# Layer A of a hybrid encoder: small products in groups, query norms from transposes, 128-row meta products, decays as rows from DRAM

## The chip, the core and the metric

The kernel runs on one core of a Trainium2 chip. The metric is the device time of one execution, in microseconds (us). The engines are PE (matmul) with its weight loads PEld, DVE (vector), ACT (scalar functions), POOL, and SP, which issues the DMAs. DRAM is the chip's large memory; SBUF and PSUM are the memories at the engines, PSUM the one that PE writes.

## The reference

The model is a trunk of two layers over 1024 tokens of width 1024 (plus 16 learned meta tokens ahead of them). Layer A is a gated delta rule with 8 heads of width 128; a shared latent key/value set is built from its output; layer B is latent attention. The change is in layer A alone:

```python
z = h @ w_in                                  # h: rms-normed input
qkv = silu(causal_dwconv(z[..., :3*1024], conv_w))
q = l2_norm(q) * 128 ** -0.5;  k = l2_norm(k)
beta = sigmoid(b_raw)
g = -exp(a_log) * softplus(a_raw + dt_bias)   # log decay per token and head
# gated_delta_rule, by chunks of tokens:
gc = cumsum(g)
decay = exp(where(tril, gc[:, None] - gc[None, :], -inf))
kb = k * beta
lower = where(tril_strict, (kb @ k.T) * decay, 0)
sol = triangular_solve(lower + eye, [v * beta, kb * exp(gc)])
attn = where(tril, (q @ k.T) * decay, 0)
# scan over chunks with the state S:
u = u_base - w_dec @ S
o = (q * exp(gc)) @ S + attn @ u
S = S * exp(gc_last) + (k * exp(gc_last - gc)).T @ u
```

Afterwards `o` is normed per head, multiplied with a gate, projected and added to the input.

## The kernel before

Tokens lie in tiles of 128, with the 16 meta tokens as a short tile ahead (tile -1, its values in column NT = 8 of the per-token tables). All float32 matmuls on weights are done as three products of split halves (`mm3`, L91 to L93, names `whi`, `wlo`, `hT_hi`, `hT_lo`). Other float32 products on 128 columns appear in the trace as two records each, transposes as one.

Layer A begins with the norm and transposition of the input (L250 to L259), the small projection for beta and decay (L264 to L287, on 32 columns of PE), and the per-token tables `beta`, `g`, `egc`, `ekd`, `egl` (L295 to L333). After that the work goes by pairs of heads. For every head, `conv_acts` makes keys, values and queries: 72 big matmuls in three chunks of tokens, and the convolution on POOL (L372) and DVE (L375). `key_prep` (L383) transposes the keys (L397), takes their squared sums on ACT, builds the decay matrix `att`, multiplies it with keys times keys (L440) into `U`, and sends `U` and the scaled betas through DRAM (`blk_in`, `beta_scr`). `invert_blocks` loads them as 66 blocks of 32x32 (`M`) and inverts them with 62 operations on DVE (L524, L527); `finish_inverses` assembles 128-row inverses with small products (names `fin`). `query_prep` takes the query norms and multiplies keys with queries. `scan_meta` and `scan_tile` run the recurrence: five products a tile and head (L611, L615, L616, L621, L625), with four results that DVE makes between them.

The decay matrix before is made by PE: for each pair of tiles POOL masks the split decay rows `ghi` and `glo` with a select (L429), PE sums them with the triangular matrix `after_r` (L431), ACT takes the exponential, and POOL selects the triangle again (L435). The query norms are sums over partitions: ACT squares the transposed queries, and PE multiplies each tile with a column of ones (L475).

The program order gives priorities, and a scheduler that works with modelled durations makes each engine's instruction list from them, so the lists interleave the pairs: the scan of one pair, the key preparation of the next and the conv matmuls of the one after share PE. Each list is executed in order. `att` has six buffers (two a head), `o`, the scan's result, three. All DMAs of layer A are issued by SP, in one queue; a DMA that waits holds up those behind it.

## Time and profile before

| | |
|---|---|
| Time, median of 3 runs | 1352.13 us (1349.76 to 1353.17) |
| Profiled execution, its own time | 1351.8 us |
| Its span | 1350.1 us |
| Mean granted TensorE clock | 0.989 |
| PE, DVE, ACT, POOL busy | 97%, 67%, 40%, 31% |

The span is the time that the profile covers; the execution's own time is 1.7 us longer. A row of a group gives the line, the engine, the operation, the output and input names, shapes and count, then busy time and the mean of one in ns, then the idle time before it and what ended it. A matmul's duration overlaps with its neighbours', so what one costs in the stream is read from the distance of starts, or from the busy time, in which overlaps are shared out.

### The profile page before, as it was taken

To read this page: it belongs to the slowest core of one execution; us is meant where nothing else is said; L and a number is where in the kernel's file an instruction comes from. 1 tells how busy PE (TensorE), PEld (TensorE's weight loads), DVE (VectorE), ACT (ScalarE), POOL (GpSimd) and SP (SyncE) were. 2 spreads that over 40 slices of the span, in tenths; PEclk is the share of its full clock that TensorE was granted. 3 is DMA by queue.
4 is the path that set the end of the run, shared out by engine and by line. 5 is a ranking of instruction groups with operands and counts; after the bars stand their busy time and mean duration, and the time that the engine had idled before them with its cause. 6 is when DMAs were issued, how large, how long until landed. Compare 5 with 4: busy or idle time off the path is not lost.

```text
span 1350.1 us, 24895 instructions
## 1 busy us (share of the span) xinstructions
PE 1306.3 (97%) x9064; PEld 1181.7 (88%) x9064; DVE 900.1 (67%) x2601; ACT 534.8 (40%) x1694; POOL 412.8 (31%) x680
## 2 busy tenths in 40 slices
PE   6999999999999999999999999998999999998998
PEld 4879989989998999997888798887999999998876
DVE  6669879968978884633553765224888878788221
ACT  6442343244325322211222243116777677776100
POOL 3344224323421320060101402212535435347000
PEclk9999999999999999999999999999999999999999
DMA  6111202111211113255441302311111101014443
GB/s 185 41 25 48 56 20 62 40 42 37 59 49 32 50 32 96 72 159 178 145 147 68 95 1 84 121 47 57 44 38 35 56 21 36 21 36 149 133 124 125
DMA packets 116924, 96.81 MB, mean 72 GB/s; under 512 B 28462, under 2 KB 106094, under 8 KB 116802
## 3 DMA queue, kind: packets, MB, share of 16 engines
q1 hardware_dynamic: 116802, 95.23, 23.7%
q8 instruction: 71, 1.16, 0.4%
q14 instruction: 51, 0.42, 0.1%
HBM read 68.19 MB, written 27.01 MB: 71 GB/s over the span
## 4 chain that ended last, share of the span: by engine, by line
PE 75%; DVE 8%; DMA 5%; POOL 5%; ACT 4%; issue 3%; SPq 0%; DVEq 0%; ACTq 0%; POOLq 0%
PE mm L91 7%; PE mm L93 7%; PE mm L92 7%; PE sc L93 6%; PE sc L92 6%; PE sc L91 6%; PE bd L91 3%; PE bd L93 3%; PE bd L92 3%; PE pt L1312 2%; PE tr L483 1%; DMA raw<-in_a_w_out 1%; ACT junk L82 1%; DMA out<-raw 1%; PE ch L625 1%
## 5 line engine op out<-in xcount | busy, mean ns | idle before, releaser
L91 PE MATMUL mm<-hT_hi,whi 128*128 128x384 f32 (+1 forms) x768 | 256.8, 334 | 3.5 <-DVE whi L98 3.5
L93 PE MATMUL mm<-hT_hi,wlo 128*128 128x384 f32 (+1 forms) x768 | 255.3, 332 | 0.7 <-DVE wlo L99 0.7
L92 PE MATMUL mm<-hT_lo,whi 128*128 128x384 f32 (+1 forms) x768 | 255.7, 333 | 0.0
L91 PEld LDWEIGHTS mm<-hT_hi,whi 128*128 128x128 f32 x768 | 147.4, 192 | 5.5 <-issue 4.7
L93 PEld LDWEIGHTS mm<-hT_hi,wlo 128*128 128x128 f32 x768 | 147.5, 192 | 2.5 <-DVE wlo L99 1.3
L92 PEld LDWEIGHTS mm<-hT_lo,whi 128*128 128x128 f32 x768 | 147.2, 192 | 1.4 <-issue 0.4
L108 DVE TENSOR_TENSOR pTl<-pt,pTh 128x256 fp32r<-128x256 f32 (+2 forms) x112 | 55.0, 494 | 11.0 <-ACT pTh L107 9.5
L98 POOL TENSOR_SCALAR whi<-raw 128x512 fp32r<-128x512 f32 x48 | 37.7, 799 | 70.4 <-PE mm L92 63.8
L82 ACT ACTIVATE P<-P,mx 128x144 f32<-128x144 f32 (+3 forms) x64 | 50.6, 791 | 21.8 <-DVE mx L1270 19.0
L91 PE MATMUL sc<-wo_hi,oTh 128*128 128x512 f32 (+1 forms) x144 | 57.5, 400 | 0.6 <-issue 0.6
L93 PE MATMUL sc<-wo_hi,oTl 128*128 128x512 f32 (+1 forms) x144 | 57.2, 397 | 0.0
L92 PE MATMUL sc<-wo_lo,oTh 128*128 128x512 f32 (+1 forms) x144 | 56.9, 395 | 0.0
L375 DVE SCALAR_TENSOR_TENSOR kn<-z,pcol,kn 128x384 f32<-128x384 f32 (+1 forms) x72 | 41.4, 576 | 19.4 <-POOL kn L372 18.8
L1283 POOL TENSOR_SCALAR P<-P,sl 128x144 f32<-128x144 f32 (+3 forms) x64 | 53.0, 829 | 3.7
L370 ACT COPY z<-mm 128x384 f32<-128x384 f32 (+1 forms) x72 | 31.8, 442 | 54.4 <-PE mm L93 54.3
L107 ACT CAST pTh<-pt 128x256 fp32r<-128x256 f32 (+2 forms) x112 | 47.3, 427 | 14.1 <-PE pt L1312 8.0
L99 DVE TENSOR_TENSOR wlo<-raw,whi 128x512 fp32r<-128x512 f32 x64 | 47.1, 746 | 8.5 <-POOL whi L98 8.4
L93 PE MATMUL sc<-h_hi,wlo 128*128 128x512 f32 x128 | 50.8, 397 | 0.0
L92 PE MATMUL sc<-h_lo,whi 128*128 128x512 f32 x128 | 50.6, 396 | 0.0
L91 PE MATMUL sc<-h_hi,whi 128*128 128x512 f32 x128 | 50.5, 395 | 0.0
L91 PE MATMUL bd<-wf_hi,oTh 128*128 128x512 f32 x128 | 50.2, 392 | 0.3 <-ACT oTh L1422 0.2
L102 DVE SCALAR_TENSOR_TENSOR wlo<-raw,pcol,whi 128x128 fp32r<-128x128 f32 x64 | 23.4, 429 | 40.0 <-POOL whi L101 40.0
(380 smaller groups left out, 3951.1 us busy)
## 6 DMA issues: line engine op xcount, KB each, us to landing
raw<-in_a_w_in SPq DMA_DIRECT2D x64, 256.0 KB
xt<-in_x SPq DMA_DIRECT2D x16, 512.0 KB
o_scr<-o SPq DMA_DIRECT2D x64, 64.0 KB
raw<-in_a_w_out SPq DMA_DIRECT2D x8, 512.0 KB
on<-o_scr SPq DMA_DIRECT2D x8, 512.0 KB
x_scr<-xt SPq DMA_DIRECT2D x8, 512.0 KB
raw<-in_b_w_in SPq DMA_DIRECT2D x8, 512.0 KB
gb_scr<-z SPq DMA_DIRECT2D x8, 512.0 KB
```

Source lines behind the costliest of these rows:

```text
L82: i = A.activation(out_ap, in_ap, func, **kw)
L91: TE.matmul(ps, ahi, bhi, start=first, stop=False)
L92: TE.matmul(ps, ahi, blo, start=False, stop=False)
L93: TE.matmul(ps, alo, bhi, start=False, stop=last)
L98: eng.tensor_scalar(out=hi, in0=raw, scalar1=1.0, scalar2=1.0, op0=ALU.mult, op1=ALU.mult)
L99: V.tensor_tensor(out=lo, in0=raw, in1=hi, op=ALU.subtract)
L107: A.copy(hi, ps)
L108: V.tensor_tensor(out=lo, in0=ps, in1=hi, op=ALU.subtract)
L370: A.copy(z[:, 3 + a:3 + b], gemm_T(hi, lo, c))
L375: V.scalar_tensor_tensor(out=yc, in0=z[:, a + j:b + j], scalar=col("cw", 24 * j + m), in1=yc, op0=ALU.mult, op1=ALU.add)
L1283: G.tensor_scalar(out=Pm[:, 0:n], in0=Pm[:, 0:n], scalar1=s, scalar2=1.0, op0=ALU.mult, op1=ALU.mult)
L1312: TE.transpose(pt[:, kb, x * P:(x + 1) * P], Ps[x][0][:, y0 + kb * P:y0 + (kb + 1) * P], ident)
```

## The change

The change touches layer A only; the part behind it has the same instructions. It does this:

- **Decays.** Instead of masked sums on PE, the sums of log decays per token are made once for all heads and tiles (`around` products), transposed, and written to DRAM (`r_scr`). Each head reads its rows back, broadcast to all partitions, into `att` (two DMAs of 256 KB a head). POOL masks it, adds the column sums `nb`, and ACT takes the exponential. The meta decays come from `rmb` and `nrm` in the same manner.
- **Query norms.** PE transposes the queries (9 products a head), and ACT squares and sums them from PSUM, as for the keys.
- **Scaled betas.** They are stored to `beta_scr` straight from their columns, 1024 pieces of four bytes a head, without transposes and copies.
- **Meta products** work on 128 rows with zeros in the rows that are not used; the small projection's weights are widened to 128 columns.
- **Order.** In `key_prep` the four transposes of a bank stand ahead of their four squares; in `scan_tile` the product with the queries stands right behind the one with the keys, and the one with `att` right behind the one with `kd`.

```diff
             sc = sp.tile([P, NT + 1], F32, tag="ksc", name=nm("ksc"))
             for half, s4 in halves() + [(2, slice(NT, NT + 1))]:
...
-                for j, t in enumerate(tiles):
-                    a, b = tok(t)
-                    TE.transpose(ps[0:k, j, :], kn[:, a:b], ident)
-                    act(junk[0:k], ps[0:k, j, :], AF.Square, accum_out=sk[0:k, s4.start + j, hc])
...
+                for j in range(n):
+                    a = tok(s4.start + j)[0] if half < 2 else 0
+                    TE.transpose(ps[:, j, :], kn[:, a:a + P], ident)
+                for j in range(n):
+                    act(junk, ps[:, j, :], AF.Square, accum_out=sk[:, s4.start + j, hc])
...
-            TE.transpose(ps[0:NT, 0:P], flat(br[:, 0:NT, hc]), ident)
-            TE.transpose(ps[0:1, P:P + NM], br[:NM, NT, hc], ident[:NM, :NM])
-            V.tensor_copy(brow, ps[0:NT, 0:P])
-            V.tensor_copy(browm, ps[0:1, P:P + NM])
-            SY.dma_start(beta_scr[h, NM:].rearrange("(t p) -> t p", p=P), brow)
-            SY.dma_start(beta_scr[hc, 0:NM], browm)
+            SY.dma_start(beta_scr[h, NM:].rearrange("(t p) -> p t", p=P), flat(br[:, 0:NT, hc]))
+            SY.dma_start(beta_scr[h, 0:NM], br[:NM, NT, hc])
...
+            for half in range(2):
+                SY.dma_start(flat(att[half]), r_scr[hc, 512 * half:512 * half + 512].broadcast_to([P, 512]))
...
             for half, s4 in halves():
-                ps = bank("tr", [P, 512])
-                for i in range(2):
-                    s2 = slice(s4.start + 2 * i, s4.start + 2 * i + 2)
-                    gs = [bp.tile([P, 2, P], F32R, tag=f"g{y}", name=nm("gm")) for y in range(2)]
-                    for y, gy in enumerate((ghi, glo)):
-                        G.affine_select(out=gs[y], in_=gy[:, s2, hc].broadcast_to([P, 2, P]), compare_op=ALU.is_ge,
-                                        fill=0.0, base=0, pattern=[[0, 2], [1, P]], channel_multiplier=-1)
-                        TE.matmul(ps[:, 256 * i:256 * i + 256], after_r, flat(gs[y]), start=y == 0, stop=y == 1)
-                act(flat(att[half]), ps, AF.Exp)
+                G.affine_select(out=att[half], in_=att[half], compare_op=ALU.is_ge, fill=MASKED, base=0,
+                                pattern=[[0, 4], [1, P]], channel_multiplier=-1)
+                a4 = att[half].rearrange("p t (c i) -> p (t c) i", c=2)
+                n4 = nb[:, h, s4].rearrange("p t c -> p (t c)")
+                G.tensor_tensor(out=a4, in0=a4, in1=n4[:, :, None].broadcast_to([P, 8, P // 2]), op=ALU.add)
+                act(flat(att[half]), flat(att[half]), AF.Exp)
...
-            for a, b in TOKC:
-                act(sq[:, a:b], qT[:, a:b], AF.Square)
-            for t in range(-1, NT):
-                a, b = tok(t)
-                s = t if t >= 0 else NT
-                TE.matmul(ps[0:b - a, s:s + 1], sq[:, a:b], one, start=True, stop=True)
+            for s4 in (slice(0, 4), slice(4, 8), slice(NT, NT + 1)):
+                ps = bank("tr", [P, 4, P])
+                junk = sp.tile([P, P], BF16, tag="jk", name=nm("junk"), bufs=1)
+                for j in range(s4.stop - s4.start):
+                    a = tok(s4.start + j)[0] if s4.start < NT else 0
+                    TE.transpose(ps[:, j, :], qT[:, a:a + P], ident)
+                for j in range(s4.stop - s4.start):
+                    act(junk, ps[:, j, :], AF.Square, accum_out=qss[:, s4.start + j:s4.start + j + 1])
...
             TE.matmul(ps[:, 0:P], c["kn"][:, a:b], S, start=True, stop=True)
+            TE.matmul(ps[:, 2 * P:3 * P], c["qT"][:, a:b], S, start=True, stop=True)
...
-            TE.matmul(ps[:, 2 * P:3 * P], c["qT"][:, a:b], S, start=True, stop=True)
...
                 TE.matmul(ps[:, 0:P], c["kd"][t // 4][:, t % 4, :], u, start=True, stop=True)
+            TE.matmul(ps[:, 3 * P:4 * P], c["att"][t // 4][:, t % 4, :], u, start=True, stop=True)
...
-            TE.matmul(ps[:, 3 * P:4 * P], c["att"][t // 4][:, t % 4, :], u, start=True, stop=True)
```

The scheduler's lists change all through layer A. PE first, in the scan of the first pair, where the keys of head 3 are transposed. In the names, `ch` are the scan's products, `mm` the conv matmuls, `tr` the others. Before:

```order
L91 MATMUL mm_473_2685<-hT_hi,whi_267_1876 128x384
L621 MATMUL ch_292_2026<-u_294_2032,kd_151_893 128x128
L397 MATMUL tr_428_2435<-ident,kn_272_1887 128x128
L92 MATMUL mm_473_2685<-hT_lo,whi_267_1876 128x384
L625 MATMUL ch_286_2008<-u_288_2014,att_108_753 128x128
L93 MATMUL mm_473_2685<-hT_hi,wlo_268_1877 128x384
L397 MATMUL tr_428_2435<-ident,kn_272_1887 128x128
L91 MATMUL mm_474_2716<-hT_hi,whi_267_1876 128x384
L397 MATMUL tr_433_2456<-ident,kn_272_1887 128x128
L92 MATMUL mm_474_2716<-hT_lo,whi_267_1876 128x384
```

And now:

```order
L92 MATMUL mm_425_2626<-hT_lo,whi_249_1879 128x384
L93 MATMUL mm_425_2626<-hT_hi,wlo_250_1880 128x384
L91 MATMUL mm_425_2626<-hT_hi,whi_249_1879 128x384
L92 MATMUL mm_425_2626<-hT_lo,whi_249_1879 128x384
L644 MATMUL ch_304_2119<-u_306_2125,kd_114_802 128x128
L645 MATMUL ch_304_2119<-u_306_2125,att_112_800 128x128
L634 MATMUL ch_310_2137<-S_301_2111,kn_107_704 128x128
L635 MATMUL ch_310_2137<-S_301_2111,qT_209_1451 128x128
L442 MATMUL tr_400_2430<-ident,kn_254_1890 128x128 x4
L93 MATMUL mm_425_2626<-hT_hi,wlo_250_1880 128x384
```

Single transposes and single scan products between the conv matmuls have become runs: four transposes, and the four scan products of two tiles, one behind the other.

SP's queue in the same scan, from the store of head 3's betas on. Before:

```order
L420 DMA beta_scr<-brow_444_2498 8x128
L631 DMA o_scr<-o_314_2092 128x128
L421 DMA beta_scr<-browm_445_2499 1x16
L631 DMA o_scr<-o_320_2110 128x128
L516 DMA bb_465_2568<-beta_scr 32x32
L518 DMA bb_465_2568<-beta_scr 1x16
L631 DMA o_scr<-o_326_2128 128x128
```

And now, from the end of head 2's betas on:

```order
L540 DMA bb_417_2509<-beta_scr 32x32
L542 DMA bb_417_2509<-beta_scr 1x16
L655 DMA o_scr<-o_302_2113 128x128
L433 DMA att_389_2401<-r_scr 128x512
L485 DMA blk_in<-U_362_2293 32x8x32
L655 DMA o_scr<-o_308_2131 128x128
L485 DMA blk_in<-U_362_2293 32x8x32 x3
L655 DMA o_scr<-o_314_2149 128x128
L486 DMA blk_in<-Um_387_2390 16x16
L433 DMA att_390_2402<-r_scr 128x512
L655 DMA o_scr<-o_320_2167 128x128
L655 DMA o_scr<-o_326_2185 128x128
```

The broadcasts into `att` of head 3 stand between the stores of `o`, each at the place where the scan frees a buffer of `att`.

More of the change, by code (lines that the diff above doesn't have):

```diff
@@ L151, in body @@
                     pattern=[[1, P]], channel_multiplier=-1)
+    around = ctile("around", [P, 2, P])
+    for c in range(2):
+        V.tensor_scalar(out=around[:, c], in0=upto, scalar1=-1.0, scalar2=None, op0=ALU.mult)
+        for q in range(1 + 2 * c):
+            r = slice(32 * q, 32 * q + 32)
+            V.tensor_scalar(out=around[r, c], in0=upto[r], scalar1=-1.0, scalar2=1.0, op0=ALU.mult, op1=ALU.add)
     one = ones[:, 0:1]
@@ L407, in key_prep @@
-            for rows, s in ((slice(0, P), slice(0, NT)), (slice(0, NM), slice(NT, NT + 1))):
-                x = lambda y: flat(y[rows, s, hc])
-                V.tensor_tensor(out=x(br), in0=x(beta), in1=x(rk), op=ALU.mult)
-                V.tensor_scalar(out=x(nbeta), in0=x(br), scalar1=-1.0, scalar2=None, op0=ALU.mult)
-                if s.start == 0:
-                    V.tensor_tensor(out=x(necb), in0=x(nbeta), in1=x(egc), op=ALU.mult)
-            ps = bank("tr", [P, 512])
-            brow = sp.tile([H, P], F32, tag="brow", name=nm("brow"))
@@ L415, in key_prep @@
[L415 to L432 removed]
+                n = s4.stop - s4.start
@@ L433, in key_prep @@
                 V.tensor_tensor(out=att[half], in0=att[half], in1=rk[:, s4, hc].broadcast_to([P, 4, P]),
                                 op=ALU.mult)
-                G.affine_select(out=att[half], in_=att[half], compare_op=ALU.is_ge, fill=0.0, base=0,
-                                pattern=[[0, 4], [1, P]], channel_multiplier=-1)
                 ps = bank("tr", [P, 512])
@@ L634, in body @@
         hs = {h: {} for h in range(H)}
+        Nms = [[bp.tile([P, P], F32, name=f"Nm{i}{hl}") for hl in range(2)] for i in range(2)]
+        for x in Nms[0] + Nms[1]:
+            G.memset(x, 0.0)
         def keys_of(h):
```

149 lines of the change are left out of this document (87 added, 62 removed).

## The prediction

> **What bounds the kernel now.** I read the page's busy shares first, then the chain of waits, the waits of PE alone, and the sums by stretch.
>
> ```profile
> PE 1306.3 (97%) x9064; PEld 1181.7 (88%) x9064; DVE 900.1 (67%) x2601; ACT 534.8 (40%) x1694; POOL 412.8 (31%) x680
> PE 75%; DVE 8%; DMA 5%; POOL 5%; ACT 4%; issue 3%; SPq 0%; DVEq 0%; ACTq 0%; POOLq 0%
> ```
>
> PE is busy for 97% of the span and holds 75% of the chain. Layer A fills roughly the first 570 us. The waits of PE in the first 760 us, longest first:
>
> ```profile
> PE tr L237 <- POOL xs L252: 8.8, 1, 8.8
> PE mm L91 <- DVE whi L98: 3.5, 2, 1.8
> PE tr L258 <- POOL xs L252: 3.2, 4, 1.5
> PE tr L431 <- POOL gm L429: 1.5, 5, 0.4
> ```
>
> The first and third are the start-up, before there is any work. After it, hardly anything makes PE wait. So in layer A the length of PE's instruction stream is the time. The sums by stretch, for the second pair of heads (columns: stretch, length, busy us and instructions of PE, PEld, DVE, ACT, POOL, then the granted clock, DMA share and GB/s):
>
> ```profile
> 180.00:225.00 45.00, 44.95 (x335) 42.29 (x335) 39.65 (x135) 17.98 (x76) 13.70 (x29) 1.00 0.20 48
> 225.00:270.00 45.00, 45.00 (x295) 43.97 (x294) 43.85 (x111) 11.28 (x26) 20.19 (x20) 0.96 0.16 43
> 270.00:295.00 25.00, 24.78 (x321) 22.10 (x320) 15.73 (x38) 10.29 (x37) 4.24 (x8) 1.00 0.24 55
> ```
>
> The first stretch is scan and key preparation, the second the conv matmuls beside the block inversion, the third the end of the inverses. PE is full in all three. But DVE has only 5.35 us of room in the first and 1.15 in the second: whatever PE gains there, DVE must be able to follow.
>
> **The change, part by part.** Groups of PE's instructions in the first 760 us (last columns: count, busy us, mean ns of one; overlapping work is shared out, so busy over count is the price of one in the stream):
>
> ```profile
> L431 PE MATMUL tr<-gm,after_r 128*128 128x256 f32 x64 | 19.5, 350 | 1.8 <-POOL gm L429 1.5
> L475 PE MATMUL tr<-ones,sq 128*128 128x1 f32 (+1 forms) x144 | 16.6, 242 | 0.0
> L416 PE MATMUL tr<-ident,br 128*8 128x128 f32 x8 | 2.2, 274 | 0.6 <-DVE br L409 0.6
> L449 PE MATMUL tr<-gmm,after 16*16 16x16 f32 x16 | 1.7, 178 | 0.0
> L417 PE MATMUL tr<-ident,br 16*1 16x16 f32 x8 | 1.4, 172 | 0.0
> L497 PE MATMUL tr<-ident,vT 128*128 128x128 f32 x64 | 9.6, 272 | 0.0
> L325 PE MATMUL tr<-g,upto 128*128 128x64 f32 x2 | 0.4, 284 | 1.0 <-DVE g L318 1.0
> L597 PE MATMUL ch<-um,kdm 16*128 16x128 f32 x16 | 3.3, 308 | 0.0
> L621 PE MATMUL ch<-u,kd 128*128 128x128 f32 x112 | 22.9, 287 | 0.0
> ```
>
> Removed from PE: the decay products (L431, 19.5 us), the query norms as products with a column of ones (L475, 16.6), the transposes of the scaled betas (L416 and L417, 2.2 + 1.4) and the meta decays (L449, 1.7): 41.4 us. Added: 72 transposes of the queries, at the price of the value transposes, 9.6 / 64 = 0.15 us each, 10.8 us; and once, in the set-up, three small products and two transposes, at about 0.2 us a record from L325, some 1.5 us. Net **-29.1 us**.
>
> The meta products go from 16 rows to 128. One of them costs 3.3 / 16 = 0.21 us now, a full-sized record of the scan 22.9 / 112 = 0.20, and both stream 128 columns: I put them at nothing, with bounds of -1 and +1 us over all heads. [...]
>
> Moved: the small products now stand together. The instruction order has 265 runs of small products between the big ones (L91 to L93) before, 116 of them a single instruction, and 193 after, 21 of them single. What a lone one costs, from the timeline of PE (start, length, instruction):
>
> ```profile
> 186.04 0.34 PE L93 MATMUL mm<-hT_hi,wlo 128*128 128x384 f32 x1
> 186.38 0.33 PE L397 MATMUL tr<-ident,kn 128*128 128x128 f32 x1
> 186.46 0.42 PE L91 MATMUL mm<-hT_hi,whi 128*128 128x384 f32 x1
> 186.73 0.34 PE L92 MATMUL mm<-hT_lo,whi 128*128 128x384 f32 x1
> ...
> 189.31 0.38 PE L625 MATMUL ch<-u,att 128*128 128x128 f32 x2
> 189.53 0.39 PE L621 MATMUL ch<-u,kd 128*128 128x128 f32 x2
> ...
> 190.04 0.34 PE L92 MATMUL mm<-hT_lo,whi 128*128 128x384 f32 x1
> 190.21 0.33 PE L93 MATMUL mm<-hT_hi,wlo 128*128 128x384 f32 x1
> 190.39 0.49 PE L625 MATMUL ch<-u,att 128*128 128x128 f32 x2
> 190.63 0.42 PE L91 MATMUL mm<-hT_hi,whi 128*128 128x384 f32 x1
> 190.89 0.38 PE L611 MATMUL ch<-S,kn 128*128 128x128 f32 x2
> ```
>
> Start to start, a big matmul behind a big one takes 0.17 (190.04 to 190.21), a pair of records in a group 0.22 (189.31 to 189.53). The lone pair at 190.39 and the big matmul behind it take 0.50 instead of 0.39: 0.11 more. The lone transpose at 186.38, with the big matmul on either side, takes 0.69 instead of 0.17 + 0.11 + 0.17: 0.24 more. So a run costs 0.11 to 0.24 us besides its work; I take 0.14, nearer to the pair, since most runs that go are pairs of the scan. 72 runs fewer are **-10 us** (bounds -8 and -17).
>
> The other engines:
>
> ```profile
> L418 DVE COPY brow<-tr 8x128 f32<-8x128 f32 x8 | 2.2, 273 | 1.5 <-PE tr L417 1.4
> L419 DVE COPY browm<-tr 1x16 f32<-1x16 f32 x8 | 1.2, 152 | 0.0
> L429 POOL TENSOR_SCALAR_AFFINE_SELECT gm<-glo 128x256 fp32r<-128x256 f32 x32 | 15.8, 495 | 0.4 <-PE tr L431 0.2
> L1188 POOL TENSOR_TENSOR t<-qraw,qC 128x128 f32<-128x128 f32 x32 | 15.9, 496 | 0.0
> L82 ACT ACTIVATE junk<-tr 128x128 bf16<-128x128 f32 (+1 forms) x72 | 19.8, 275 | 22.8 <-PE tr L397 21.9
> L82 ACT ACTIVATE sq<-qT 128x384 f32<-128x384 f32 (+1 forms) x24 | 10.9, 488 | 0.2
> L252 POOL TENSOR_SCALAR xs<-xt,ss 128x1024 f32<-128x1024 f32 (+1 forms) x9 | 10.0, 1119 | 10.2 <-DMA prow<-in_k_gain 3.5 <-DMA raw<-in_a_w_in 2.3 <-issue 1.6
> ```
>
> DVE loses the row copies (2.2 + 1.2 us) and three small operations a head that were done apart for the 16 meta rows, 5 to 6 us in all, about 1.3 a pair. POOL loses 64 selects (L429 has two groups of 32) and gains 16 additions over 128x512, 4 x 0.496 = 2.0 us each by size: 32 for about 31, even. ACT squares the queries in 72 pieces instead of 24: about 20 us for 11, with ACT at 18 of 45 us in the stretch above. Neither is on the path.
>
> Two things take back. First DVE. A pair gains 39 / 4 = 9.8 us of PE. In the 90 us from 180 to 270 DVE has 6.5 us idle and loses 1.3 of work, so a pair that became 9.8 us shorter there would leave it none (6.5 + 1.3 = 7.8); what falls to the third stretch is free. I charge 2 us a pair, **+8** (bounds 0 and +20). Second the set-up: a fill of 128x1024 on POOL between the first input scalings (1.1 us as L252) and six small DVE operations, **+2**.
>
> The decay rows now come by DMA: 16 broadcasts of 256 KB and, before them, one store. The betas go out as 1024 pieces of four bytes instead of 8 rows. SP's queue, from its timeline:
>
> ```profile
> 75.39 0.25 SPq L421 DMA_DIRECT2D beta_scr<-browm  x1
> 76.31 0.31 SPq L516 DMA_DIRECT2D bb<-beta_scr  x1
> ...
> 81.97 1.80 SPq L461 DMA_DIRECT2D blk_in<-U  x4
> ```
>
> And a load of 264 KB from the chain of waits:
>
> ```profile
> 335.56 3.78 DMA M<-blk_in
> ```
>
> The read of the betas waits 0.92 us for their store. Four stores of 256 pieces take 1.80 us, 1.8 ns a piece, so 1024 pieces go out in about 1.8 too. The broadcasts are the size of M's load, 3.78 us. SP's stores of o stand behind these waits; o has three buffers and a tile of one head leaves every 45 / 16 = 2.8 us, so some 6 us are covered. I charge nothing; bounds 0 and +5 us for each of the 8 stores.
>
> [...]
>
> Sum: -29.1 - 10 + 8 + 2 = -29. The profiled execution took 1351.8 us (0.3 below the median), so **1323 us**.
>
> **Rivals.** *All of PE's gain arrives*: DVE's idle time proves movable and a run costs 0.24. For it: PE waits on DVE for 3.5 us of weights alone. Against: 43.85 of 45. -29 - 17 + 2 = -44: 1308 us. *DVE becomes the bound in scan and inversion alike*: each pair gains only its 6.5 + 1.3 us of DVE room less the imbalance, about half of 9.8: 39 - 20 = 19, less 2 and less some late inverse, 1337 us. For it the second stretch; against it the third, where DVE has 9 us free. *The SP queue stalls the scan (slower)*: the four-byte store lands late, the read of the betas and the stores of o stand behind it, the scan lacks a buffer for o, DVE stops in order and PE behind it. Covered up to 6 us a store; to end above 1356 it must eat 33 us, so about 10 us a store over 8 stores; at 12 us, 1323 + 8 x 6 = 1371. Against it: the 256-piece stores. *No gain*: the set-up and the late first inverse eat what the rest brings, 1350 us; PE's row sums speak against it.
>
> **How the numbers follow.** Forecast 0.47 (1313 to 1331), all of the gain 0.20, half of it 0.20, no change 0.05, slower 0.08. A measurement of this kernel tells about 0.3% from no change (its runs spread over 0.25%), so below 1348 counts as faster: 0.87, same 0.05, slower 0.08. The range of 1304 to 1345 holds the first three but for a tail of about 0.07 below it.
>
> **What would show it.** In the profile after, L431's and L475's kind are gone and PE's busy time falls by 25 to 40 us, with DVE's share in 180 to 270 at 95% or more. The key transposes stand in runs of four, 0.11 us apart. Wrong would be: PE's waits grow by 10 us or more on DVE or DMA; SP's wait between the store of the betas and their read is over 6 us; or big matmuls still take 0.26 us beside small ones, and the runs cost the same as before.

## The result, and the profile after

The changed kernel takes **1387.78 us** (median of 4 runs, 1382.44 to 1390.43) against 1351.83 for the kernel before in the same measurement: ratio 1.0262, 95% interval 1.0227 to 1.0298. It is slower by about 36 us, where 29 us less were forecast, and it lies outside the range of 1304 to 1345. The profiled execution took 1386.22 us, its span is 1384.5, its mean granted clock 0.978 (before: 1350.1 and 0.989).

The page of the changed kernel, busy shares and the chain of waits by engine:

```profile
PE 1286.9 (93%) x8904; PEld 1183.9 (86%) x8904; DVE 902.0 (65%) x2577; ACT 548.5 (40%) x1814; POOL 410.2 (30%) x631
PE 64%; DVE 13%; DMA 8%; POOL 6%; ACT 6%; issue 4%; SPq 0%; POOLq 0%; DVEq 0%; ACTq 0%
```

PE lost 160 records and 19.4 us of busy time, so the work did leave PE. But PE's share of the chain fell from 75% to 64%, and DVE, DMA, POOL and ACT all hold more of it. The three stretches of layer A that were full before (columns as there):

```profile
180.00:225.00 45.00, 39.73 (x303) 38.97 (x298) 31.64 (x126) 19.03 (x81) 7.03 (x10) 0.92 0.16 34
225.00:270.00 45.00, 39.50 (x239) 38.54 (x238) 34.93 (x84) 8.54 (x23) 22.29 (x22) 0.92 0.25 63
270.00:295.00 25.00, 21.30 (x138) 20.66 (x137) 21.93 (x55) 10.65 (x45) 9.32 (x11) 0.93 0.19 51
```

PE now stands for over 5 us of each 45, DVE has not become full either (31.64 and 34.93, before 39.65 and 43.85), and the granted clock is 0.92 and 0.93, where it was 1.00, 0.96 and 1.00. Nobody is busy, and PE is slower when it runs. What PE waits for between 60 and 620 us (total, times, longest):

```profile
PE tr L470 <- DVE kd L448: 20.7, 5, 5.9
PE tr L507 <- ACT junk L82: 15.2, 7, 4.1
PE ch L639 <- DVE r L637: 13.1, 3, 4.4
```

Behind the third stands a wait of DVE for a free buffer of `o`, whose store has not landed:

```profile
DVE o L651 <- DMA o_scr<-o: 14.9, 3, 5.0
```

None of these waits of PE was there before, where PE's longest wait behind the start-up was 1.8 us. One of the stops of the first kind can be followed back through four engines, in their timelines (start, length, instruction, in brackets the wait ahead of it and who ended it). PE, DVE, ACT, POOL, then SP's queue:

```profile
210.84 1.20 PE L470 MATMUL tr<-kn 128*128 128x128 f32 x4 [5.27 <-DVE kd L448]
```

```profile
209.93 0.16 DVE L182 TENSOR_TENSOR nt<-ny 128x1 f32<-128x1 f32 x1 [5.35 <-ACT ny L82]
210.01 0.68 DVE L448 TENSOR_TENSOR kd<-tr,ksc 128x512 f32<-128x512 f32 x1
```

```profile
208.65 0.63 ACT L82 ACTIVATE att<-att 128x512 f32<-128x512 f32 x1 [6.75 <-DMA att<-r_scr]
209.48 0.19 ACT L82 ACTIVATE ny<-ns 128x1 f32<-128x1 f32 x1
```

```profile
206.41 0.63 POOL L459 TENSOR_SCALAR_AFFINE_SELECT att<-att 128x512 f32<-128x512 f32 x1 [18.14 <-DMA att<-r_scr]
```

```profile
192.91 0.39 SPq L455 DMA_DIRECT2D beta_scr<-br  x1
...
194.37 0.32 SPq L655 DMA_DIRECT2D o_scr<-o  x1
200.33 0.32 SPq L540 DMA_DIRECT2D bb<-beta_scr  x1
...
202.40 0.38 SPq L433 DMA_DIRECT2D att<-r_scr  x1
```

And SP's waits of that kind from 60 to 620 us:

```profile
SPq L540 <- DMA beta_scr<-br: 50.1, 7, 9.2
```

Read the timelines from the bottom. The betas leave at 192.91 in 1024 pieces. The read of the betas stands at the head of SP's queue until they have landed, so nothing is issued between 194.7 and 200.33 and the read goes out 7.4 us after the store. The broadcast of the decay rows goes out at 202.40 and POOL gets it at 206.41. ACT, which works in order, has stood 6.75 us at the exponential of that tile, and a small reciprocal root (`ny`, for the key norm of the short tile) stands behind it. DVE waits for it, the scaled keys `kd` wait behind that on DVE, and so a PSUM bank is not freed, for which PE waits at the key products. Three in-order lists pass one late transfer on to PE.

The DMA engines are not busy in that time. In the rows of the stretch (the last two numbers are the DMA share and GB/s) the packets run between 193 and 196, and then none runs at all until the read goes out:

```profile
193.00:196.00 3.00, 3.00 (x25) 2.94 (x24) 2.35 (x10) 0.40 (x2) 0.00 (x0) 1.00 0.32 45
196.00:200.30 4.30, 4.30 (x36) 4.30 (x35) 4.01 (x16) 2.90 (x18) 0.00 (x0) 1.00 0.00 0
```

So the pieces are sent in about 2 us, and SP's wait for them ends nearly 6 us later. What happens to the writes in between, the trace does not show. The chain of waits shows other transfers that land late, a store of `o` for one (the second number is the us to its landing):

```profile
220.76 10.70 DMA o_scr<-o
```

### The profile page after: what moved, and what is told of

It is laid out like the page before. It is cut to its first block, busy times and chain, and to the rows that moved or that the text cites. A ratio compares the mean times of both kernels' runs of the same rounds, so it can differ in the third digit from the quotient of the medians.

```text
span 1384.5 us, 24699 instructions
## 1 busy us (share of the span) xinstructions
PE 1286.9 (93%) x8904; PEld 1183.9 (86%) x8904; DVE 902.0 (65%) x2577; ACT 548.5 (40%) x1814; POOL 410.2 (30%) x631
## 4 chain that ended last, share of the span: by engine, by line
PE 64%; DVE 13%; DMA 8%; POOL 6%; ACT 6%; issue 4%; SPq 0%; POOLq 0%; DVEq 0%; ACTq 0%
PE sc L93 6%; PE sc L92 6%; PE sc L91 6%; PE bd L91 4%; PE bd L93 4%; PE mm L93 4%; PE bd L92 4%; PE mm L91 4%; PE mm L92 4%; DMA o_scr<-o 2%; ACT junk L82 2%; DVE qT L418 2%; PE pt L1340 2%; PE tr L507 1%; DMA att<-r_scr 1%
## 5 line engine op out<-in xcount | busy, mean ns | idle before, releaser
L98 POOL TENSOR_SCALAR whi<-raw 128x512 fp32r<-128x512 f32 x48 | 46.6, 980 | 74.5 <-PE mm L92 61.3
L418 DVE SCALAR_TENSOR_TENSOR kn<-z,pcol,kn 128x384 f32<-128x384 f32 (+1 forms) x72 | 44.9, 624 | 16.0 <-POOL kn L415 15.3
L548 DVE TENSOR_TENSOR tmp<-M 66x31 f32<-66x31 f32 (+15 forms) x124 | 47.3, 382 | 6.7 <-POOL bb L538 5.0
L92 PE MATMUL bd<-wf_lo,oTh 128*128 128x512 f32 x128 | 49.8, 389 | 0.0
```

The costliest lines, as they stand in the source:

```text
L92: TE.matmul(ps, ahi, blo, start=False, stop=False)
L98: eng.tensor_scalar(out=hi, in0=raw, scalar1=1.0, scalar2=1.0, op0=ALU.mult, op1=ALU.mult)
L418: V.scalar_tensor_tensor(out=yc, in0=z[:, a + j:b + j], scalar=col("cw", 24 * j + m), in1=yc, op0=ALU.mult, op1=ALU.add)
L548: V.tensor_tensor(out=tv, in0=M[:, k, k + 1:32][:, :, None].broadcast_to([66, m, w]), in1=M[:, k:k + 1, 0:w].broadcast_to([66, m, w]), op= ...
```

## The experiments

All were timed in three rounds beside the kernel before on the same chip. "Clock" is the mean granted clock over a kernel's runs. A span times its clock is taken as the span at the full clock, and the rest as what the clock took. That is bookkeeping, not a cost in the strict sense, since half a clock in a stretch in which PE waits may cost nothing; but it separates two effects that the time mixes. The runs of one kernel scatter by 0.6 to 4.5 us in span times clock and by 1.3 to 8.2 in the clock's part (one standard deviation). The median of the kernel before moved between 1351.2 and 1353.1 from one group of runs to the next, so a difference of medians between kernels of different groups is good to some 2 us.

| Kernel | median us | ratio to before, 95% | clock | span x clock | taken by the clock |
|---|---|---|---|---|---|
| before (70 runs) | 1351 to 1353 | | 0.989 | 1336.1 | 14.8 |
| the change | 1387.8 | 1.0227 to 1.0298 | 0.975 | 1350.4 | 35.0 |
| e1 change, row store | 1358.2 | 1.0030 to 1.0075 | 0.981 | 1330.9 | 25.5 |
| e2 before, 4-byte store | 1366.4 | 1.0076 to 1.0150 | 0.984 | 1342.1 | 22.5 |
| e3 change, 32-byte store, 4-byte reads | 1356.3 | 1.0028 to 1.0057 | 0.980 | 1327.8 | 27.1 |
| e4 change, late reads | 1385.4 | 1.0164 to 1.0279 | 0.970 | 1340.4 | 41.1 |
| e5 before, grouping | 1355.2 | 1.0005 to 1.0059 | 0.980 | 1327.6 | 27.4 |
| e6 before, new query norms | 1366.9 | 1.0060 to 1.0127 | 0.982 | 1339.6 | 24.3 |
| e7 = e1, old query norms | 1355.9 | 0.9992 to 1.0030 | 0.983 | 1330.1 | 23.1 |
| e8 = e1, old decays | 1353.2 | 0.9977 to 1.0014 | 0.987 | 1335.3 | 17.0 |
| e9 less PE work | 1330.6 | 0.9818 to 0.9886 | 0.986 | 1311.3 | 19.0 |
| e10 less DVE work | 1358.4 | 1.0031 to 1.0068 | 0.985 | 1336.9 | 20.0 |
| e11 less of both | 1327.4 | 0.9786 to 0.9847 | 0.986 | 1306.9 | 18.2 |
| e12 = e3, query norms later | 1359.0 | 1.0029 to 1.0080 | 0.982 | 1333.1 | 24.4 |
| e13 before, new decays | 1346.8 | 0.9942 to 0.9970 | 0.990 | 1331.4 | 13.3 |
| e14 before, cheap query norms | 1344.9 | 0.9935 to 0.9967 | 0.990 | 1330.2 | 13.3 |
| **e15 = e13 + e14** | **1336.1** | 0.9869 to 0.9904 | 0.993 | 1325.3 | 9.3 |
| e16 change, store on ACT's queue | 1391.2 | 1.0274 to 1.0315 | 0.973 | 1351.6 | 38.2 |
| e17 = e1, pieces as well | 1386.7 | 1.0220 to 1.0276 | 0.975 | 1350.5 | 35.0 |
| e18 = e15, e3's store | 1345.3 | 0.9909 to 0.9956 | 0.989 | 1328.8 | 14.8 |

### The store of the betas: e1, e2, e3, e4, e16, e17

e1 is the changed kernel with the store as it was before:

```diff
-SY.dma_start(beta_scr[h, NM:].rearrange("(t p) -> p t", p=P), flat(br[:, 0:NT, hc]))
-SY.dma_start(beta_scr[h, 0:NM], br[:NM, NT, hc])
+TE.transpose(ps[0:NT, 0:P], flat(br[:, 0:NT, hc]), ident)      # and the meta row
+V.tensor_copy(brow, ps[0:NT, 0:P])
+SY.dma_start(beta_scr[h, NM:].rearrange("(t p) -> t p", p=P), brow)
```

> The changed kernel with one part undone: the scaled betas go to DRAM as before (two transposes, two row copies, a store of 8 rows and one of 1). Theory A (the store of 1024 four-byte pieces lands 7 to 11 us late and holds up SP's queue and the DMAs behind it, and this is where the time went): SP's waits on the store, 50.1 us in the changed kernel, fall under 10, PE's waits in layer A fall from about 56 to under 20, and the time is 1315 to 1345 us. Theory B (the decay rows that come by broadcast DMA, with ACT in order behind them, are the cause): the time stays at 1370 us or more. Theory C (the query squares on ACT hold PSUM banks): at most 10 us off, 1378 or more.

e2 is the same edit the other way round, in the kernel before:

> The kernel before with one part of the change alone: the scaled betas are stored straight from their columns in four-byte pieces, without the transposes and the row copies. Theory A: 8 waits of some 7 us stand in SP's queue, and the time goes up by 20 to 45 us, to 1372 to 1397. Theories B and C: the removed transposes and copies save 2 to 7 us of PE and DVE, and the time is 1345 to 1355.

Measured: 1358.2 and 1366.4. Both lie between the ranges that were named. Inside the change the store costs 1387.8 - 1358.2 = 30 us, alone in the kernel before some 15. SP's waits between the store and the read, of e1 and then of e2, with what DVE waits for in e2 (60 to 620 us):

```profile
SPq L547 <- DMA beta_scr<-brow: 1.4, 4, 0.6
```

```profile
SPq L509 <- DMA beta_scr<-br: 44.2, 7, 9.6
DVE o L620 <- DMA o_scr<-o: 9.4, 4, 3.6
```

SP waits 0.6 us at most for the eight rows, up to 9.6 for the 1024 pieces. The DVE row is the mechanism of the third rival: no free buffer for `o`, because its store has not landed. But e1 is still 7 us above the kernel before, not 29 below, so the store explains less than half of the miss of 65 us (1323 forecast).

e3 asks whether small pieces cost as much in reads:

```diff
+V.tensor_copy(brc, flat(br[:, 0:NT, hc]))
+SY.dma_start(beta_scr[h, NM:].rearrange("(p t) -> p t", t=NT), brc)     # 128 pieces of 32 bytes
 ...
+by_q = beta_scr[g0 + hl, NM:].rearrange("(q i t) -> q t i", q=4, t=NT)
+SY.dma_start(bb[33 * hl + q:33 * hl + 32:4, :], by_q[q])                # four reads, 4-byte pieces
```

> The changed kernel with the transposition of the betas moved from the store to the read: one small DVE copy a head, a store of 128 pieces of 32 bytes, and four reads of 256 four-byte pieces where there was one of 32 pieces. Theory A with slow landing of small writes: the store lands within 2 to 3 us, reads in small pieces cost little, and the time is 1320 to 1350. Theory A with any four-byte piece being slow: the read is late in its place and the inversion waits for it, 1365 or more. Theories B and C: no change, 1375 to 1395.

Measured 1356.3, as e1, between the two ranges of its theory A. SP waits 0.2 us for this store, in one wait. So in this kernel neither 128 written pieces of 32 bytes nor 1024 read pieces of four bytes show a loss like that of the 1024 written ones; for the reads e18 below is less clear. e4 leaves the store and moves only the read, behind the load of `M`, so that SP does not stand at the head of its queue:

```diff
-SY.dma_start(flat, blk_in[gi].rearrange("p a b -> p (a b)"))
+mload = SY.dma_start(flat, blk_in[gi].rearrange("p a b -> p (a b)"))
+with tc.issue_after(mload.ins):      # the two reads of beta_scr into bb stand in here now
```

> The changed kernel with its four-byte stores, but the reads of the betas are issued behind the load of M, so that SP does not stand waiting for the store with other DMAs behind it. If the harm is SP's wait at the head of its queue: 1320 to 1350. If the harm is that the DMAs behind the store (the stores of o, the broadcasts) land late because they share its rings: 1360 or more, with DVE still waiting for stores of o. Theories B and C: no change, 1375 to 1395.

Measured 1385.4 (1372.1 to 1390.3). SP's waits for the store fall from 50.1 to some 11 us, and PE's stops for `kd` from 20.7 to 5.9, so that wait did reach PE. But the time does not follow. In its chain a store of `o` still takes 10.1 us to land (at 350.36), and a broadcast that is issued 0.5 us behind the pieces reaches POOL 14 us later, where it took 4 above (202.40 to 206.41); PE's longest stop, 10.5 us, follows from it:

```profile
SPq L485 <- DMA beta_scr<-br: 6.9, 2, 4.3
SPq L656 <- DMA beta_scr<-br: 4.3, 1, 4.3
```

```profile
465.69 0.37 SPq L455 DMA_DIRECT2D beta_scr<-br  x1
466.15 0.53 SPq L433 DMA_DIRECT2D att<-r_scr  x1
```

```profile
480.23 0.63 POOL L459 TENSOR_SCALAR_AFFINE_SELECT att<-att 128x512 f32<-128x512 f32 x1 [14.19 <-DMA att<-r_scr]
```

e16 issues both stores of the betas from ACT's queue:

```diff
-SY.dma_start(beta_scr[h, NM:].rearrange("(t p) -> p t", p=P), flat(br[:, 0:NT, hc]))
+A.dma_start(beta_scr[h, NM:].rearrange("(t p) -> p t", p=P), flat(br[:, 0:NT, hc]))
```

> The changed kernel as it is, with the two stores of the betas issued on ACT's queue instead of SP's. The betas land as late as before this edit, but the stores of o and the broadcasts of the decay rows no longer stand behind 1024 pieces on the same queue. If what costs some 30 us is what stands behind the store on its queue: 1355 to 1365. If it is the late betas (late inverses, late scan), or the pieces hold up the DMA engines for every queue: 1380 to 1390.

Measured 1391.2, and in its chain of waits a store of `o`, which still goes by SP's queue, lands as late as before:

```profile
220.25 11.38 DMA o_scr<-o
```

So a store need not stand behind the pieces in one queue to land late. SP's own wait at the read stays in this kernel (59.2 us in 7 waits, up to 12.3), so the run does not tell what that wait costs. e17 sends the betas in rows, and the pieces go to a spare tensor:

```diff
 SY.dma_start(beta_scr[h, NM:].rearrange("(t p) -> t p", p=P), brow)
 SY.dma_start(beta_scr[hc, 0:NM], browm)
+SY.dma_start(junk_scr[h, NM:].rearrange("(t p) -> p t", p=P), flat(br[:, 0:NT, hc]))
```

> The changed kernel with the betas stored in rows, as before (1358.2 in its own runs), and behind them, once a head, the 1024 pieces of four bytes as well, into a spare tensor that nothing reads. The betas are there in time. If the late betas cost the 30 us: 1356 to 1362, as without the pieces. If the pieces hold up every other transfer (stores of o, blocks for the inverses, broadcasts): 1380 to 1392, with stores of o landing 10 us late again.

Measured 1386.7, as the change. The pieces do it though nobody reads them. The scheduler placed them ahead of the rows on SP, and the betas were not there in time after all, as SP's timeline and its waits show:

```profile
217.13 0.37 SPq L465 DMA_DIRECT2D junk_scr<-br  x1
...
219.11 0.29 SPq L463 DMA_DIRECT2D beta_scr<-brow  x1
...
230.11 0.32 SPq L549 DMA_DIRECT2D bb<-beta_scr  x1
```

```profile
SPq L549 <- DMA beta_scr<-brow: 50.2, 8, 8.1
```

Eight rows, for which SP waits 0.6 us in e1, take 11 us when they are issued 2 us behind the pieces. So in these runs what is issued within some microseconds behind the pieces lands late, from the same queue or another: rows here, stores of `o` in the change and e16, a broadcast in e4. How much of the 30 us goes by way of the late betas, with SP standing at their read, and how much by the late stores of `o` and broadcasts, no run separates; that stays open.

### The parts alone: e5, e6, e13, e7, e8

e5 is the kernel before with only the grouping (key transposes ahead of the squares, L615 moved to L611, L625 to L621, and L600 ahead of its copy):

```diff
                     TE.transpose(ps[0:k, j, :], kn[:, a:b], ident)
+                for j, t in enumerate(tiles):
                     act(junk[0:k], ps[0:k, j, :], AF.Square, accum_out=sk[0:k, s4.start + j, hc])
...
             TE.matmul(ps[:, 0:P], c["kn"][:, a:b], S, start=True, stop=True)
+            TE.matmul(ps[:, 2 * P:3 * P], c["qT"][:, a:b], S, start=True, stop=True)
```

> The kernel before, with nothing changed but the order of the small products: key transposes ahead of their squares, the two products of a scan step that share an input side by side. My prediction's term: -10 us (bounds -8 and -17), so 1341 us (1334 to 1343). Rival (the runs cost nothing that can be won, or the later start of the squares costs as much): 1348 to 1354. A third reading, that the grouping delays the chain of the scan, gives over 1355.

Measured 1355.2: no gain. But the PE work did fall. Of PE's groups in the first 760 us, key transposes and first scan product, of the kernel before and then of e5:

```profile
L397 PE MATMUL tr<-ident,kn 128*128 128x128 f32 x64 | 18.7, 305 | 0.7 <-ACT junk L82 0.7
L611 PE MATMUL ch<-S,kn 128*128 128x128 f32 x128 | 24.1, 281 | 0.0
```

```profile
L397 PE MATMUL tr<-ident,kn 128*128 128x128 f32 x64 | 10.7, 293 | 0.0
L612 PE MATMUL ch<-S,kn 128*128 128x128 f32 x128 | 27.0, 295 | 0.0
```

The transposes lose 8 us and the first scan product gains 3 (all five of them 5.5); the big matmuls lose 4 (767.8 to 764.0). In the table span times clock falls by 8.5 us, near the forecast of 10, and the clock takes 12.6 back. The half-clock stretches in its trace last up to 10.2 us, in the kernel before none is longer than 3.4. (The profiled execution was the longest of the ten, with a clock of 0.974.)

e6 is the kernel before with only the new query norms, as the change has them:

```diff
-act(sq[:, a:b], qT[:, a:b], AF.Square)                                       # 3 a head
-TE.matmul(ps[0:b - a, s:s + 1], sq[:, a:b], one, start=True, stop=True)      # 9 a head
+TE.transpose(ps[:, j, :], qT[:, a:a + P], ident)                             # 9 a head
+act(junk, ps[:, j, :], AF.Square, accum_out=qss[:, s4.start + j:s4.start + j + 1])
```

> The kernel before, with only the query norms taken from transposes. By the sum of the prediction: 16.6 us of products go and 10.8 us of transposes come, -6 us, 1346. Rival (ACT's 72 squares hold the banks of PSUM, and the products of keys and queries stand on PE behind them; that wait was 13 to 15 us in all kernels with the new norms): +5 to +12 us, 1357 to 1364, with a wait of PE at the key-query products on ACT's squares of over 8 us that the kernel before doesn't have.

Measured 1366.9: the rival's sign and its wait, at a price above its range of 1357 to 1364. PE's wait, and then the stretches around one handover from inverses to scan, first of e6, then of the kernel before (columns as above; the third number from the end is the granted clock):

```profile
PE tr L483 <- ACT junk L82: 13.4, 7, 3.8
```

```profile
285.00:294.00 9.00, 8.02 (x151) 6.82 (x148) 6.97 (x13) 4.71 (x15) 2.63 (x4) 1.00 0.27 66
294.00:308.00 14.00, 14.00 (x92) 12.74 (x90) 4.57 (x14) 4.84 (x18) 1.01 (x2) 0.51 0.01 2
```

```profile
285.00:294.00 9.00, 8.78 (x158) 7.37 (x158) 4.66 (x21) 5.88 (x20) 0.59 (x2) 1.00 0.13 32
294.00:308.00 14.00, 13.88 (x121) 12.07 (x120) 11.29 (x37) 5.71 (x22) 6.03 (x13) 1.00 0.06 14
```

With less than a microsecond more of standing PE, the next 14 us run at half the clock: 92 records instead of 121, while the row still calls PE 100% busy. Here a busy PE is a slow PE. The squares themselves, in the changed kernel (ACT, first 760 us, keys and queries together), and two of them in e6's timeline of ACT:

```profile
L82 ACT ACTIVATE junk<-tr 128x128 bf16<-128x128 f32 x144 | 39.8, 276 | 20.9 <-PE tr L442 16.4 <-PE tr L498 1.3
L82 ACT ACTIVATION_READ_ACCUMULATOR junk<-tr 128x1 f32 x144 | 28.1, 195 | 0.0
```

```profile
256.48 0.28 ACT L82 ACTIVATE junk<-tr 128x128 bf16<-128x128 f32 x1
...
256.88 0.28 ACT L82 ACTIVATE junk<-tr 128x128 bf16<-128x128 f32 x1
```

A square with a sum is two instructions, 0.276 and 0.195 us long, which overlap a little: start to start it takes 0.40. So the 72 of the queries are some 29 us of ACT, not 20. Four of them hold a bank for some 1.6 us, and PE's next products need that bank.

e13 has only the new decays: of the change it keeps `r_scr`, `nb`, `rmb` and the 128 rows of the meta products, and takes back the store, the grouping and the query norms.

> The kernel before with the new decays alone (rows broadcast from DRAM, the new meta decays and their 128 rows): no grouping, query norms as products with ones, betas stored in rows. PE loses the decay products, 14.4 us start to start and 1.1 for the meta decays. If this removal arrives as it did where nothing came in its place (36 us removed, 21.5 gained, so 0.6): -9, 1343. If the broadcasts, POOL's additions and ACT's order eat it: 1350 to 1358, with waits of PE of 10 us and more that the kernel before does not have.

Measured 1346.8, clearly faster, though far from the 15 us that PE no longer does. In its profiled run, the longest of the ten, PE's busy time is 14.9 us less than before (1291.4) and PE stands for 12.4 us more, spread over small waits, the largest sum of which is 3.4 us. POOL's addition, in the changed kernel, costs 1.1 us each:

```profile
L463 POOL TENSOR_TENSOR att<-att,nb 128x512 f32<-128x512 f32 x16 | 17.5, 1097 | 0.6
```

e7 is e13 with the grouping (that is, e1 with the lines of e6 taken back); e8 is e1 with the decays taken back (the meta decays stay new):

```diff
-SY.dma_start(flat(att[half]), r_scr[hc, 512 * half:512 * half + 512].broadcast_to([P, 512]))
-G.tensor_tensor(out=a4, in0=a4, in1=n4[:, :, None].broadcast_to([P, 8, P // 2]), op=ALU.add)
+TE.matmul(ps[:, 256 * i:256 * i + 256], after_r, flat(gs[y]), start=y == 0, stop=y == 1)
```

> The changed kernel with the betas stored in rows as before and the query norms from squares of qT and products with ones, as before. Left of the change: decays from broadcast rows, grouping, 128 rows for the meta products. If ACT's squares of the queries are what ate the gain: well below the 1358 of the one with row stores alone, 1335 to 1342. If the broadcast decays are: 1355 to 1365, about as with the new norms or above.

> The changed kernel with the betas stored in rows and the decays of the 128-token tiles from PE products as before (the meta decays stay new). Left of the change: query norms from transposes, grouping, 128 rows. PE does 19.5 us more than in the one with row stores alone. If the broadcast decays cost nothing off PE, as the prediction has it: 1358 + 19 = 1377. If their chain (broadcast, POOL select and addition, exp in ACT's order) is what ate the gain: 1345 or less.

Measured 1355.9 and 1353.2, against 1358.2 with all parts. On top of the new decays the grouping costs 9 us by the medians, 7 by the ratios, all of it clock (13.3 to 23.1). The parts do not add. e5 and e6 alone lose some 3 and 13 us; e8, which has both and the 128 rows, nothing. The new query norms cost 13 us in the kernel before and only 2 to 5 on top of e7. The new decays gain 5.5 alone and lose 5 on top of e8, which fits neither of e8's forecasts (1377; 1345 or less). Why, the runs do not show.

### Where the bound is: e9, e10, e11

> The kernel before, without the decay products and their selects (the decays are one exp of a nearly constant input) and without the query norms (their products and squares; a constant stands in their place). PE has 36 us less to do (19.5 + 16.6) and nothing comes in their place on any engine. By the prediction PE's stream is the time: -36, 1317, or -30, 1323, by the start-to-start sums (14.4 + 15.5). Rival, DVE as near to its limit as PE (102 us busy in a pair of heads of 116 to 124 us): most of it turns into waits of PE, 1335 to 1350.

> The kernel before, without one of the three additions of taps that DVE does in the convolution (the last tap is left out): 126 / 3 = 42 us less for DVE, PE's work unchanged. If PE's stream alone is the time, nothing: 1349 to 1354. If DVE is the bound in places that PE's busy share hides: 1325 to 1340.

> The kernel before without the decay products, without the query norms and without the last tap: 36 us less on PE, 42 less on DVE. If the PE stream alone is the time, the same as without the PE work alone. If DVE takes back what PE gives, this one gets it: 1310 to 1322, and 15 us or more below the one with less PE work alone.

The edits: the decay products and selects give way to `act(flat(att[half]), kn[:, ...], AF.Exp, scale=1e-3, bias=low)`, the query norms to a `memset` of 1; and `range(1, 4)` over the taps becomes `range(1, 3)`. Measured 1330.6, 1358.4 and 1327.4. PE's stream is the bound, as the prediction had it: taking work off PE gains 21.5 us. Taking an addition of taps off DVE (42 us by the rows, 27 of its busy time on the page, since neighbours overlap) gains nothing; it is 6 slower, which was not followed up, and the scheduler also chose another order. Taking both gains only 3 more than PE alone. But only 21.5 of 36 arrive, and e9, e10 and e11 all lie beside the ranges that were named. A piece of the rest is in e9's timeline of PE, with ACT's behind it:

```profile
154.25 0.33 PE L399 MATMUL tr<-ident,kn 128*128 128x128 f32 x1 [3.57 <-ACT junk L82]
```

```profile
153.04 0.52 ACT L82 ACTIVATE kn<-kn 128x384 f32<-128x384 f32 x1 [3.25 <-DVE kn L377]
```

PE waits 12.0 us in 4 such stops. ACT is not at work in this one: it stands 3.25 us for DVE's convolution of the keys, its squares stand behind that in its list, and PE's key transpose needs the bank that they free. Big matmuls stand behind the transpose in PE's list and cannot start. So with less work PE runs into the pace of DVE and ACT here.

### A better way to the same ends: e12, e14, e15, e18

e12 is e3 with the block of `qss` (query transposes, squares, `epsq`) moved from ahead of the key-query products to behind them.

> The changed kernel with the betas copied, stored in pieces of 32 bytes and read in pieces of four bytes (1356.3 in its own runs), and now with the query transposes and their squares behind the key-query products instead of ahead of them. If the wait of PE at these products (14.7 us in 8) for ACT's squares to leave the PSUM banks is a real part of the loss: it goes, and its half-clock windows with it, 1340 to 1346. If it only moves to the next user of a bank, or DVE sets the pace anyway: 1352 to 1358.

Measured 1359.0, e3's time or a little more. The wait moved and grew (in e3 it was 14.7 us in 8):

```profile
PE tr L510 <- DVE att L499: 19.5, 9, 4.5
```

e14 leaves the query norms where they are and makes the products cheap, by the type of `sq` and of the ones (with two columns of ones):

```diff
-sq = kp.tile([P, L], F32, tag="vT", name=nm("sq"), bufs=1)
+sq = kp.tile([P, L], F32R, tag="vT", name=nm("sq"), bufs=1)
-TE.matmul(ps[0:b - a, s:s + 1], sq[:, a:b], one, start=True, stop=True)
+TE.matmul(ps[0:b - a, 2 * s:2 * s + 2], sq[:, a:b], one_r, start=True, stop=True)
```

> The kernel before with only one thing changed: the squares of the queries and the column of ones are written in the packed type of the large products, so that the 144 products of the query norms (15.5 us start to start) are cheaper, while ACT's three squares a head and every other step stay where they are. If PE's stream is the time there and ACT needs no new work: -5 to -8, 1344 to 1347. If these products only stood in time in which PE would have waited for ACT and DVE anyway: 1350 to 1354.

> The new decays alone and the cheaper query norms together: the sum of the two above. 1336 if both arrive; 1350 to 1356 if neither does.

Measured 1344.9 and 1336.1. The products, in e14's groups of PE, take 9.6 us instead of 16.6 (one record each instead of two), and the time falls by 7:

```profile
L477 PE MATMUL tr<-one_r,sq 128*128 128x2 f32 x64 | 8.3, 250 | 0.0
L477 PE MATMUL tr<-one_r,sq 128*16 128x2 f32 x8 | 1.3, 166 | 0.0
```

**e15 beats both kernels**: 1336.1 us, ratio 0.9886 (0.9869 to 0.9904), with the highest clock of all. Its longest wait of PE:

```profile
PE tr L519 <- DVE epsq L509: 7.1, 4, 2.4
```

e18 is e15 with the edit of e3, which takes 16 small transposes off PE.

> The version with the new decays and the cheaper query norms (1336.1 in its own runs), and the betas copied by DVE, stored in pieces of 32 bytes and read in pieces of four, so that their 16 small transposes and the wait for them leave PE. By the rows 1.6 us of transposes and DVE's row copies go: 1333 to 1335. If reads of four bytes cost like the writes: over 1345.

Measured 1345.3, just inside the branch in which reads cost like the writes: 9 us worse by the medians, 6 by the ratios, and the clock is 5.5 of the 9. POOL waits 12 us in all for landings of these reads, 7.3 in one wait:

```profile
POOL vT L417 <- DMA bb<-beta_scr: 7.3, 1, 7.3
```

Whether that is the cause was not followed up; in e3, where no engine waits for these reads, the same edit stood level with the row store.

## Why the prediction was wrong, step by step

- **"After it, hardly anything makes PE wait. So in layer A the length of PE's instruction stream is the time."** Right for the kernel before, in that work off PE gains and work off DVE does not (e9, e10). It fails as a rule for the price of removed work: of 36 us by the rows (19.5 + 16.6) 21.5 arrived with nothing in their place. What was left out is that a PE with less to do comes up against the other engines (12.0 us of stops behind ACT and DVE in e9).
- **"I charge nothing; bounds 0 and +5 us for each of the 8 stores."** The largest single error. It is about +30 us, 3.7 us a store, inside the bounds of this term; but eight times 5 is 40 us, and the range that ended at 1345 did not carry them. The count of pieces was priced by issue (1.8 us, from pieces of another size); the issue took 0.39, and the time to land was not priced at all. The third rival had the store, its sign, its way and nearly its price: about 10 us late, of which some 6 are covered, is 4 us net a store. SP's wait at the read occurs (50.1 us in 7, up to 9.2), and so does DVE's for a buffer of `o` (14.9 us in 3). What the rival lacked is that transfers behind the pieces land 10 to 14 us late also where SP does not stand at the read (e4) or where the pieces are in another queue (e16). Why the four-byte pieces land late, no run shows; the store of e3, in 128 pieces of 32 bytes, was not late (SP waits 0.2 us for it).
- **"ACT squares the queries in 72 pieces ... Neither is on the path."** Wrong. In time ACT had room, in order it did not: PE waits 13 to 15 us for banks (e6 and the change). The term of -6 us (10.8 - 16.6 at PE) became +13. The size was off too: 29 us of ACT and not 20, since the sum of a square is an instruction of its own. On top of the other parts the new norms cost less, 2 to 5 us (e7).
- **"72 runs fewer are -10 us."** Right in PE's work (-8.5 us at the full clock in e5), wrong in the time (+2 by the medians). The failed step is tacit: that PE time saved is time saved at the same clock.
- **Decays, 19.5 + 1.7 us of PE, their additions "even" on POOL.** Right in sign, a quarter of the size: -5.5 us (e13), and a loss on top of the other parts (e8). In e13 most of what PE no longer does turns into small waits of PE; that they come from ACT standing in order for POOL and the broadcast, as in the changed kernel at 208.65, is not shown. POOL's addition takes 1.1 us, not the 2.0 estimated.
- **"DVE takes back 2 a pair, +8."** Too dear by what e11 shows: it is 3 us below e9, and their runs overlap.
- **128 rows "at nothing", set-up +2.** Not tested apart. In the rows of e13 the three meta products take 9.5 us against 9.0 before, inside the bounds, and the fill on POOL in the changed kernel takes 1.0, as estimated.
- **The clock was in no term.** It overlaps with the terms above, and by the bookkeeping it is large: 20 of the 36 us go with it (35.0 - 14.8), give or take 4 by the scatter of the four runs. Of the change's sum, -29 in the forecast, the parts without the pieces give -5 at the full clock and +11 by the clock (e1); the pieces give +20 and +9.5.

Of the signs named beforehand, PE's waits grew by over 10 us on DVE and SP waits over 6 us between store and read, both named as signs against; PE's busy time fell by 19.4 us and not by 25 to 40, and DVE is at 70 to 78% in 180 to 270, not at 95. The third sign against, that runs cost the same as before, did not come: grouping does take work off PE (e5). Of the 65 us between forecast and result 30 are the pieces. The other 35 lie in the query norms, the grouping and the decays; since the parts do not add, the runs do not split them further.

## What to carry to other kernels

When PE is full, the work to take off it is that which nothing else has to make up for: the same products in a cheaper type gained all of their 7 us, while handing them to ACT with a PSUM bank in between lost 13 (e6), though ACT was busy for only 40% of the span. In a kernel with in-order lists, price a new step by what stands behind it in each list, and a DMA by when it lands and not by its issue: a store in four-byte pieces delayed what was issued behind it, from two queues (eight rows on the same queue landed 11 us late in e17, a store of `o` on another 11.4 us after its issue in e16). And look at the granted clock beside the time: in e6 a gap of 1.0 us stands ahead of 13.7 us at half clock.

## What the runs showed of the hardware that was not expected

- 1024 writes of four bytes are issued in 0.4 us on SP and sent in about 2, and the read that waits for them goes out 7 us and more after the issue (192.91 to 200.33), with the DMA engines idle for 4.3 us of it; a store of eight rows issued 2 us behind them lands 11 us later (e17), a store of 64 KB on another queue 11.4 us after its own issue (e16). Reads in pieces of four bytes show no loss like it in e3; in e18 they may.
- In the traces of both kernels the granted clock is 1.0 or 0.5, in stretches of 1 to 118 times 3.41 us (but for the last, which the end of the trace cuts off). Before, nine stretches at half clock make 31 us of the span, none longer than 3.4; in the changed kernel fifteen make 62, the longest 6.8; in e5 it is some 71 by its clock (0.974 over 1363.9 us). In the changed kernel ten of the fifteen stretches begin inside waits of PE of 3.5 to 5.9 us or at most 0.8 us behind them. But shorter waits came with it too: ahead of each of the eight stretches of 10 to 17 us that begin at the handover from inverses to scan (e1, e2, e5, e6, e8), PE had stood for 0.7 to 1.7 us at the first product of the meta tokens. And the wait alone does not decide: in the changed kernel waits of 3.5 us (ended at 535.83), 2.6 (961.62) and 1.2 (797.69) are followed by no half clock in the next 8 us and more. In the kernel before, four stretches come with no gap at all: PE is 100% busy in the 6.9 us ahead of each. One of them, and what filled the last 2 us ahead of it, products of one column each:

```profile
125.00:128.40 3.40, 3.40 (x28) 3.13 (x27) 2.91 (x6) 0.43 (x1) 2.99 (x3) 1.00 0.24 69
128.40:131.80 3.40, 3.40 (x17) 3.27 (x16) 3.33 (x10) 1.63 (x4) 0.68 (x1) 0.50 0.00 0
```

```profile
126.34 2.08 PE L475 MATMUL tr<-ones,sq 128*16 128x1 f32 x18
```

  PE is 100% busy in both rows. Of the eight places with these products five have a stretch at half clock behind them, begun at most 1.1 us after their end; three have none. Whether these products bring it, no run tests.
